# One-pass first gate/up products, and earlier or later lanes around them, in a hybrid decoder layer

## The chip, the cores and the metric

The kernel runs on one core of a Trainium2 chip. The metric is the time of one execution on the device in microseconds (us). The core has five engines that this text names as the profile does: PE (TensorE, matrix products), DVE (VectorE), ACT (ScalarE), POOL (GpSimd) and SP (SyncE, which here only issues DMAs). Each engine works through its own list of instructions in order, and waits on semaphores where an instruction needs another engine's result or a landed DMA. Results of PE arise in banks of PSUM, the accumulators' memory, which the kernel takes as tiles of 128x512 float32 (four for `mm`, three for `tr`, one for `ct`).

## The reference

The reference is one decoder layer on a sequence of 2048 tokens of 1024 numbers, in float32:

```python
hn = rms_norm(h, mix_pre_g)
proj = hn @ w_in                      # q, k, v and the convolution group's input u
attn_out = sliding_window_attention(q, k, v, attn_sinks, rel_bias)   # window 128, 8 query heads, 2 kv heads
conv_out = conformer_conv(u, ...)     # GLU, causal depthwise conv of width 31, layer norm, silu, @ w_conv_pw
mixed = concatenate([attn_out, conv_out]) @ w_out
h = h + rms_norm(mixed, mix_post_g)
hn = rms_norm(h, ffn_pre_g)
ff = (silu(hn @ w_gate) * (hn @ w_up)) @ w_down        # 2816 hidden columns
h = h + rms_norm(ff, ffn_post_g)
```

## The kernel before

**Tiles and groups.** The sequence is cut into four tiles of 512 tokens, numbered 0 to 3. Letters mark the stages: A is the input projection of a tile, B its attention, C the convolution and its tail, J a product of weights (w_conv_pw with the lower half of w_out, so that the convolution's output meets one matrix `w_join` instead of two), W the output projection with the norms behind it, H the turned and scaled input of the feed-forward part, F the gate and up products, G the down products with the last norm. F and G work on two groups of two tiles each (group 0: tiles 0 and 1; group 2: tiles 2 and 3), and their products are done by a Strassen scheme with seven block products instead of eight: of a group's input, B11 and B21 are the two halves of its first tile's columns, and T1 to T4 and B22 are sums and differences with the second tile.

**float32 by three products.** Every float32 operand is split into a rounded part and a rest: ACT copies the rounded part (`act(..., AF.Copy)`), and DVE or POOL subtracts it for the rest (`lo`). One block product with 512 inner terms is four times three matmuls of 128x128 by 128x512, twelve in all, in one PSUM bank.

**The first gate/up pass.** `stage_pre` does the Strassen terms that need only a group's first tile, while the second tile is still on its way. For each of PRE = 20 (group 0) or 16 (group 2) weight matrices, alternately of w_gate and w_up, there is a first half, product with B11, and a second half, product with B21. Before the change all first halves run, then all second halves: the result of a first half is copied by ACT to SBUF (`u`, L965) and stored to HBM (`keep`, L966, on ACT's DMA queue). For its second half it is loaded back (`fetch`, L926, on SP's queue, into one of two `gb` tiles), and ACT copies it into a fresh PSUM bank (`seed`, L941), onto which PE adds the twelve matmuls of the second half. Of a gate matrix, ACT then takes silu (L970), and of an up matrix DVE multiplies. The stored first halves are also needed later, in the pass `stage_p1`, which loads all of them again.

**What sets the order.** The main line (A0 to A3, then F and G of group 0, F and G of group 2) is written as generators that yield a cost in us of PE, and lanes beside it (lists of other generators, with the condition under which each may start) are advanced at the yields: a lane for attention, one for the convolution tails and J, one for W0 to W3, one for H (`lh`). Each engine's list comes out of this and of a reordering by a cost model. `lh.until("B21.0")` drives the H lane until a named operand is written.

**The lanes in the places that the change touches.** `stage_join` loads six pairs of matrices in turn into the one tile `wx`, and splits them, for eight plus four products. `stage_w(0, ...)` starts when A3 has started and the convolution tail C0 is done. `stage_h_plain` turns tile 0's (or 2's) normed rows by PE transposes into bank `tr`, of which there are three, shared with attention; it reads the rows by DMA from `hn_scr`, where the norm at the end of W stores them. `stage_h_sums` does the same with the second tile and forms T1 to T4 and B22 (S0 and S2 below); it is started at product PRE_S0 = 22 or PRE_S2 = 16 of the pass. The tails of the convolution, C2 and C3, which run in the pass G of group 0, load four rows of `y_scr` one by one, each just ahead of its turning on PE.

Of the kernel before, what the change touches and what calls it, by code (L numbers as in the profile page):

```python
# [25 lines left out]
P = 128  # L26
# [11 lines left out]
def layer_kernel(ctx, tc, x, xT, cols, rows, sinks, relb, onehot, w_in, w_pw, w_out, w_gate, w_up, w_down, out):  # L38
# [539 lines left out]
    def stage_tail(t):  # L578
        L = f"C{t}"
        lab[0] = L  # L580
        yt = t_("yt", (P, 4, 4 * P))
        ycs = []
        turn = turner(yt, ycs)
        for c in range(4):
            lab[0] = L
            y = f2("fc")
            nc.sync.dma_start(y, y_scr[c, :, t * T : (t + 1) * T])
            ycs.append(y)
            turn(c)
            yield 0.5  # L590
        yield from conv_tail(t, yt)
# [28 lines left out]

    def stage_join():
        lab[0] = "J0"
        right = []
        for k in range(4):
            raw = f4("wx", (P, 2, T))
            nc.sync.dma_start(raw, w_out[4 + k].rearrange("p (a b) -> p a b", a=2))
            yield JL
            for n in range(2):
                lab[0] = "J0"
                right.append(split_w(raw[:, n], "mid" if k < 2 else "chl"))  # L630
            yield 1.5
            lab[0] = "J0"
        for mp in range(2):
            pair_ = t_("yt", (P, 2, 2, T), F32R)
            raw = f4("wx", (P, 2, T))
            nc.sync.dma_start(raw, w_pw[2 * mp : 2 * mp + 2].rearrange("m p t -> p m t"))
            yield JL
            lab[0] = "J0"
            left = [split_w(raw[:, m], pair_[:, m]).rearrange("p a (k c) -> p a k c", c=P) for m in range(2)]
# [74 lines left out]
    def stage_w(w, spill, G, atag, htag, mtag, bank_of, norm=None):  # L714
# [13 lines left out]
        stage = t_("mb", (P, 2, T)) if w == 1 else None  # L728
# [14 lines left out]
        for gi in range(KC // G):  # L743
            aa = nxt
            for n in range(2):
                lab[0] = L
                if n == 0 and gi + 1 < KC // G:
                    if w == 1 and G * gi + G == 4:
                        ld.until("C1")
                        lab[0] = L  # L750
                    rows_next = load(gi + 1)
# [94 lines left out]
    def stage_h_plain(ws, ops, n, off):  # L846
        L = f"H{ws[0]}"
        for k in range(4):
            lab[0] = L
            b = turned(ws[0], k + off, tr, COLTAG[ws[0]][k] if ws[0] else "fa")  # L850
# [53 lines left out]
    def stage_pre(ws, ops, mid, keep, q0=0, q1=None):  # L904
        PRE = PRES[ws[0]]
        q1 = q1 or 2 * PRE
        L = f"F{ws[0]}"
        raws = {}
        wops = {}
        kept = {}  # L910

        def load(q):
            if q < q1 and q % 2 == 0:
                lab[0] = L
                half, m = divmod(q, PRE)
# [5 lines left out]

        def fetch(q):
            if PRE <= q <= q1:
                lab[0] = L
                kept[q] = f2("gb")
                nc.sync.dma_start(kept[q], keep[q - PRE if q < q1 else 0])  # L926

        def split(q):
            if q < q1:
# [5 lines left out]
        seeded = {}  # L935

        def seed(q):
            if PRE <= q < q1:
                lab[0] = L
                seeded[q] = mm()  # L940
                act(seeded[q], kept.pop(q), AF.Copy)  # L941

        load(q0)
        load(q0 + 2)
        for q in range(q0, q0 + 3):
            split(q)
        for q in range(q0, q1):
            half, m = divmod(q, PRE)
# [6 lines left out]
            if q + 2 == PRE:  # L955
                fetch(q + 2)
            lab[0] = L
# [3 lines left out]
            o = seeded.pop(q) if half else mm()  # L961
            product(o, wops.pop(q), ops[bn], not half)
            if not half:
                u = f2("fa")
                act(u, o, AF.Copy)  # L965
                nc.scalar.dma_start(keep[m], u)  # L966
            else:
# [7 lines left out]
        early[ws[0]] = kept.pop(q1)  # L975
# [321 lines left out]
    class Lane:  # L1297
# [36 lines left out]
        def until(self, name):  # L1334
            while name not in self.done:
                assert self.items, name
                n, gen, needs = self.items[0]
                assert not needs or needs(), n
                inlane[0] = True
                for c in gen:  # L1340
                    assert c is not None
                inlane[0] = False
# [15 lines left out]
    PRES = {0: 20, 2: 16}  # L1358
    POOL_LO = (3, 6)
# [3 lines left out]
    JL = 10  # L1363
# [24 lines left out]
    lw.add("W0", stage_w(0, True, 2, "x", "hl", "fa", mm), lambda: "A3" in started and "C0" in ld.done)  # L1388
# [139 lines left out]
```

## Time and profile before

| | us |
|---|---|
| time, median of 3 runs (range) | 1991.51 (1990.13 to 1993.91) |
| profiled execution: its time | 1997.53 |
| profiled execution: its span | 1995.6 |
| PE busy | 1940.2 (97%) |
| DVE busy | 1488.0 (75%) |
| ACT busy | 970.8 (49%) |
| POOL busy | 331.1 (17%) |

The profiled execution is one run with the hardware's recorder on; its span runs from the first to the last instruction, and its time has 1.9 us more. It was 6.0 us longer than the median of the three runs without a recorder. Busy time is the time in which an engine has an instruction in work; "idle before, releaser" says how long an engine stood still ahead of a group of instructions, and which instruction of which other engine, or which DMA, ended that. PEld is the loading of the weights for a matmul, which runs beside the matmul before. PEclk is the clock that PE was granted, as a share of the full one. In the trace, the first gate/up pass of group 0 runs from about 568.8 to 702 us, that of group 2 from 1343.5 to about 1440 us; W1 ends at 569, J, W0 and the attention lie before, and the tails C2 and C3 between 1015 and 1343 us.

### The profile page before, as it was taken

To read this page: it belongs to the slowest core of one execution; us is meant where nothing else is said; L and a number is where in the kernel's file an instruction comes from. 1 tells how busy PE (TensorE), PEld (TensorE's weight loads), DVE (VectorE), ACT (ScalarE), POOL (GpSimd) and SP (SyncE) were. 2 spreads that over 40 slices of the span, in tenths; PEclk is the share of its full clock that TensorE was granted. 3 is DMA by queue.
4 is the path that set the end of the run, shared out by engine and by line. 5 is a ranking of instruction groups with operands and counts; after the bars stand their busy time and mean duration, and the time that the engine had idled before them with its cause. 6 is when DMAs were issued, how large, how long until landed. Compare 5 with 4: busy or idle time off the path is not lost.

```text
span 1995.6 us, 26899 instructions
## 1 busy us (share of the span) xinstructions
PE 1940.2 (97%) x8730; PEld 1546.2 (77%) x8730; DVE 1488.0 (75%) x2679; ACT 970.8 (49%) x1910; POOL 331.1 (17%) x395
## 2 busy tenths in 40 slices
PE   8999999899999999999999999999899999999998
PEld 6877677667777788878878878778688888888886
DVE  5998989955884899988759985675866665555557
ACT  5355334456566643333355446476544333345443
POOL 6001311231111300000000020003523332311000
PEclk9999999999999999999999999999999999999999
DMA  8786654567859876787477687689834442366654
GB/s 311 256 310 217 219 167 143 186 214 253 276 176 332 298 253 239 233 278 260 162 266 245 231 280 270 195 303 353 307 139 169 169 153 101 126 220 212 211 185 159
DMA packets 234364, 452.99 MB, mean 227 GB/s; under 512 B 23496, under 2 KB 49264, under 8 KB 234224
## 3 DMA queue, kind: packets, MB, share of 16 engines
q1 hardware_dynamic: 212592, 415.63, 61.8%
q10 hardware_dynamic: 19392, 28.32, 3.9%
q0 software_dynamic: 2240, 7.34, 1.0%
q8 instruction: 68, 1.11, 0.2%
q14 instruction: 72, 0.59, 0.1%
HBM read 330.08 MB, written 121.12 MB: 226 GB/s over the span
## 4 chain that ended last, share of the span: by engine, by line
PE 76%; DMA 9%; DVE 8%; issue 3%; ACT 3%; POOL 1%; SPq 0%; ACTq 0%; DVEq 0%; POOLq 0%
PE mm@F L108 30%; PE mm@G L108 18%; PE mm@A L108 14%; PE mm@W L108 4%; PE tr@W L108 4%; PE tr@B L108 3%; DMA gb@F<-keeps 2%; DVE fc@C L85 1%; PE ct@J L108 1%; DVE mid@W L85 1%; DMA mixT<-fc@C 1%; DVE w@F L85 1%; DMA chl@F<-w_up 1%; DVE fa@F L85 1%; DVE chl@F L85 1%
## 5 line engine op out<-in xcount | busy, mean ns | idle before, releaser
L85 DVE SCALAR_TENSOR_TENSOR fc@C<-glu@C,colt,fc@C 128x512 f32<-128x512 f32 x480 | 367.9, 782 | 2.4
L108 PE MATMUL mm@F<-hl@H,w@F 128*128 128x512 f32 x1056 | 254.2, 390 | 4.3 <-ACT mm@F L941 4.3
L108 PE MATMUL mm@G<-hl@G,hl@G 128*128 128x512 f32 x924 | 227.4, 397 | 7.4 <-ACT mm@G L1232 2.9
L108 PEld LDWEIGHTS mm@F<-hl@H,w@F 128*128 128x128 f32 x1056 | 197.5, 188 | 47.0 <-ACT mm@F L941 6.2
L108 PE MATMUL mm@A<-hl@A,w@A 128*128 128x512 f32 x840 | 209.4, 398 | 2.6 <-DVE hl@A L85 1.3
L108 PEld LDWEIGHTS mm@G<-hl@G,hl@G 128*128 128x128 f32 x924 | 173.5, 190 | 46.5 <-ACT mm@G L1232 3.4
L108 PE MATMUL mm@G<-w@G,hl@G 128*128 128x512 f32 x876 | 199.7, 389 | 0.0
L814 ACT ACTIVATE w@F<-chl@F 128x512 fp32r<-128x512 f32 x220 | 135.0, 624 | 118.6 <-PE mm@F L108 112.8
L108 PEld LDWEIGHTS mm@G<-w@G,hl@G 128*128 128x128 f32 x876 | 164.3, 188 | 34.4 <-issue 0.3
L108 PEld LDWEIGHTS mm@A<-hl@A,w@A 128*128 128x128 f32 x840 | 156.8, 190 | 40.6 <-DVE hl@A L85 3.0
L85 DVE TENSOR_TENSOR w@F<-chl@F,w@F 128x512 fp32r<-128x512 f32 x198 | 145.2, 735 | 39.0 <-ACT w@F L814 38.8
L108 PE MATMUL mm@F<-mid@H,w@F 128*128 128x512 f32 x528 | 132.3, 394 | 7.9 <-ACT mm@F L941 7.3
L108 PE MATMUL mm@F<-p@H,w@F 128*128 128x512 f32 x528 | 130.6, 393 | 0.0
L108 PE MATMUL mm@F<-ql@H,w@F 128*128 128x512 f32 x528 | 127.1, 390 | 2.0 <-ACT w@F L814 2.0
L108 PE MATMUL mm@F<-x@H,w@F 128*128 128x512 f32 x528 | 126.8, 391 | 1.0 <-DVE x@H L85 0.9
L108 PEld LDWEIGHTS mm@F<-mid@H,w@F 128*128 128x128 f32 x528 | 98.1, 188 | 31.4 <-ACT mm@F L941 9.6
L108 PEld LDWEIGHTS mm@F<-ql@H,w@F 128*128 128x128 f32 x528 | 98.9, 188 | 23.0 <-ACT w@F L814 2.6
L108 PEld LDWEIGHTS mm@F<-p@H,w@F 128*128 128x128 f32 x528 | 100.1, 190 | 21.3 <-ACT at@F L1068 0.4
L108 PEld LDWEIGHTS mm@F<-x@H,w@F 128*128 128x128 f32 x528 | 98.3, 188 | 23.4 <-DVE x@H L85 1.4
L108 PE MATMUL mm@W<-w@W,hl@W 128*128 128x512 f32 x384 | 106.0, 415 | 7.4 <-ACT hl@W L723 5.6
L133 ACT ACTIVATE w@A<-raw@A 128x512 fp32r<-128x512 f32 x110 | 67.4, 626 | 73.9 <-PE mm@A L108 46.1
L85 DVE TENSOR_TENSOR w@G<-raw@G,w@G 128x512 fp32r<-128x512 f32 x73 | 51.2, 701 | 67.6 <-ACT w@G L814 66.6
(301 smaller groups left out, 3307.6 us busy)
## 6 DMA issues: line engine op xcount, KB each, us to landing
mids<-fa@F SPq DMA_DIRECT2D x154, 256.0 KB, 2.7
raw@A<-w_in SPq DMA_DIRECT2D x55, 512.0 KB, 4.4
w@A<-lo_in SPq DMA_DIRECT2D x84, 256.0 KB, 3.4
fc@G<-mids SPq DMA_DIRECT2D x77, 256.0 KB, 3.3
fa@G<-mids SPq DMA_DIRECT2D x75, 256.0 KB, 4.8
gb@F<-keeps SPq DMA_DIRECT2D x74, 256.0 KB, 4.5
w@W<-lo_out SPq DMA_DIRECT2D x48, 256.0 KB, 4.2
chl@F<-w_gate SPq DMA_DIRECT2D x22, 512.0 KB, 3.9
```

The lines of the kernel that those rows point to most:

```text
L85: r = op(*args, **kw)
L108: r = nc.tensor.matmul(*args, **kw)
L133: act(w[:, 0], raw, AF.Copy)
L814: act(w[:, 0], x, AF.Copy)
```

## The change

**The pass.** `TWO` says how many matrices of a group still have their halves in two rounds; it is 0 for both groups, so all go through in pairs: first half of matrix m, first half of m+1, second half of m, second half of m+1. The seed of a second half is no longer loaded from HBM: ACT copies it from the bank of the first half into a fresh bank, right behind the copy `u`. `u` is stored to HBM as before. The last `fetch`, of the first stored half, which `stage_p1` begins with, stays.

**J** loads its matrices one ahead, by turns into `wx` and a spare `mb` tile that W1 later uses. **W0** starts when J is done; C0 is asked for inside W0, where its second half begins. **H of group 0** turns its rows in bank `ct` (one bank, the convolution tail's) instead of `tr`. **C2 and C3** load their first two rows ahead of turning, and each further row one step ahead.

```diff
@@ -581,14 +581,30 @@
+        if t > 1:
+            yield from ahead(L, t, ycs)
         for c in range(4):
             lab[0] = L
+            if c == len(ycs):
+                y = f2("fc")
+                nc.sync.dma_start(y, y_scr[c, :, t * T : (t + 1) * T])
+                ycs.append(y)
+            turn(c)
+            if t > 1 and c < 2:
+                y = f2("fc")
+                nc.sync.dma_start(y, y_scr[c + 2, :, t * T : (t + 1) * T])
+                ycs.append(y)
+                yield 3
+            else:
+                yield 0.5
+        yield from conv_tail(t, yt)
+
+    def ahead(L, t, ycs):
+        for c in range(2):
             y = f2("fc")
             nc.sync.dma_start(y, y_scr[c, :, t * T : (t + 1) * T])
             ycs.append(y)
-            turn(c)
-            yield 0.5
-        yield from conv_tail(t, yt)
+        yield 6
 
...
+    spare = []
+
+    def spare_tile():
+        if not spare:
+            spare.append(t_("mb", (P, 2, T)))
+        return spare[0]
+
     def stage_join():
         lab[0] = "J0"
+        srcs = [w_out[4 + k].rearrange("p (a b) -> p a b", a=2) for k in range(4)]
+        srcs += [w_pw[2 * m : 2 * m + 2].rearrange("m p t -> p m t") for m in range(2)]
+        raws = {}
+
+        def load(i):
+            if i < len(srcs):
+                lab[0] = "J0"
+                raws[i] = spare_tile() if i % 2 else f4("wx", (P, 2, T))
+                nc.sync.dma_start(raws[i], srcs[i])
+
+        load(0)
+        load(1)
+        yield JL
         right = []
         for k in range(4):
-            raw = f4("wx", (P, 2, T))
-            nc.sync.dma_start(raw, w_out[4 + k].rearrange("p (a b) -> p a b", a=2))
-            yield JL
             for n in range(2):
                 lab[0] = "J0"
-                right.append(split_w(raw[:, n], "mid" if k < 2 else "chl"))
-            yield 1.5
+                right.append(split_w(raws[k][:, n], "mid" if k < 2 else "chl"))
+            yield JS
+            load(k + 2)
+            yield JS
+        for mp in range(2):
             lab[0] = "J0"
-        for mp in range(2):
             pair_ = t_("yt", (P, 2, 2, T), F32R)
-            raw = f4("wx", (P, 2, T))
-            nc.sync.dma_start(raw, w_pw[2 * mp : 2 * mp + 2].rearrange("m p t -> p m t"))
-            yield JL
-            lab[0] = "J0"
-            left = [split_w(raw[:, m], pair_[:, m]).rearrange("p a (k c) -> p a k c", c=P) for m in range(2)]
+            left = [split_w(raws[4 + mp][:, m], pair_[:, m]).rearrange("p a (k c) -> p a k c", c=P) for m in range(2)]
             yield 2
             for m in range(2):
                 for n in range(2):
@@ -725,7 +756,7 @@
-        stage = t_("mb", (P, 2, T)) if w == 1 else None
+        stage = spare_tile() if w == 1 else None
 
...
                 if n == 0 and gi + 1 < KC // G:
-                    if w == 1 and G * gi + G == 4:
-                        ld.until("C1")
+                    if w < 2 and G * gi + G == 4:
+                        ld.until(f"C{w}")
...
-            b = turned(ws[0], k + off, tr, COLTAG[ws[0]][k] if ws[0] else "fa")
+            b = turned(ws[0], k + off, tr if ws[0] else ct, COLTAG[ws[0]][k] if ws[0] else "fa")
...
-    def stage_pre(ws, ops, mid, keep, q0=0, q1=None):
-        PRE = PRES[ws[0]]
-        q1 = q1 or 2 * PRE
+    def stage_pre(ws, ops, mid, keep):
+        PRE, two = PRES[ws[0]], TWO[ws[0]]
         L = f"F{ws[0]}"
-        raws = {}
-        wops = {}
-        kept = {}
+        seq = [(m, half) for half in range(2) for m in range(two)]
+        for m in range(two, PRE, 2):
+            seq += [(m + j, half) for half in range(2) for j in range(2)]
+        raws, wops, kept, seeded = {}, {}, {}, {}
 
         def load(q):
-            if q < q1 and q % 2 == 0:
-                lab[0] = L
-                half, m = divmod(q, PRE)
+            if q < len(seq) and q % 2 == 0:
+                lab[0] = L
+                m, half = seq[q]
                 raw = t_("raw", (P, 2, T))
                 for j in range(2):
                     src, pr = MATS[m + j]
                     nc.sync.dma_start(raw[:, j], src[2 * pr][:, half * T : (half + 1) * T])
                     raws[q + j] = raw[:, j]
 
+        def stored(q):
+            return q == len(seq) or q < len(seq) and seq[q][1] and seq[q][0] < two
+
         def fetch(q):
-            if PRE <= q <= q1:
+            if stored(q):
                 lab[0] = L
                 kept[q] = f2("gb")
-                nc.sync.dma_start(kept[q], keep[q - PRE if q < q1 else 0])
+                nc.sync.dma_start(kept[q], keep[seq[q][0] if q < len(seq) else 0])
 
         def split(q):
-            if q < q1:
+            if q < len(seq):
                 lab[0] = L
                 raw = raws.pop(q)
                 wops[q] = split_f(raw, hl("w"))
                 lo(raw, wops[q], ws[0] and q % 2 == 1)
 
-        seeded = {}
-
         def seed(q):
-            if PRE <= q < q1:
-                lab[0] = L
-                seeded[q] = mm()
-                act(seeded[q], kept.pop(q), AF.Copy)
-
-        load(q0)
-        load(q0 + 2)
-        for q in range(q0, q0 + 3):
+            if q < len(seq) and stored(q):
+                lab[0] = L
+                seeded[seq[q][0]] = mm()
+                act(seeded[seq[q][0]], kept.pop(q), AF.Copy)
+
+        load(0)
+        load(2)
+        for q in range(3):
             split(q)
-        for q in range(q0, q1):
-            half, m = divmod(q, PRE)
+        for q, (m, half) in enumerate(seq):
             started.add(f"P{ws[0]}.{q}")
             bn = "B21" if half else "B11"
             if len(ops.get(bn, ())) < 4:
                 lh.until(f"{bn}.{ws[0]}")
             split(q + 3)
             load(q + 4)
-            if q + 2 == PRE:
+            if stored(q + 2) and not stored(q + 1):
                 fetch(q + 2)
-            lab[0] = L
             seed(q + 1)
             fetch(q + 3)
             lab[0] = L
-            o = seeded.pop(q) if half else mm()
+            o = seeded.pop(m) if half else mm()
             product(o, wops.pop(q), ops[bn], not half)
             if not half:
                 u = f2("fa")
                 act(u, o, AF.Copy)
                 nc.scalar.dma_start(keep[m], u)
+                if m >= two:
+                    seeded[m] = mm()
+                    act(seeded[m], o, AF.Copy)
             else:
...
-        early[ws[0]] = kept.pop(q1)
+        early[ws[0]] = kept.pop(len(seq))
...
                 assert not needs or needs(), n
+                was = inlane[0]
                 inlane[0] = True
...
-                inlane[0] = False
+                inlane[0] = was
...
     PRES = {0: 20, 2: 16}
+    TWO = {0: 0, 2: 0}
...
-    JL = 10
+    JL, JS = 10, 2
...
-    lw.add("W0", stage_w(0, True, 2, "x", "hl", "fa", mm), lambda: "A3" in started and "C0" in ld.done)
+    lw.add("W0", stage_w(0, True, 2, "x", "hl", "fa", mm), lambda: "A3" in started and "J" in ld.done)
```

The first place is in the pass of group 2, on ACT. Before, its rows are (`raw` is a weight matrix as loaded, `w` its split, `gb` a half that was loaded back, `fa` the copy to be stored, `keeps` the store in HBM):

```order
L941 ACTIVATE mm@F_2232_12930<-gb@F_2227_12907 128x512
L965 ACTIVATE fa@F_2220_12877<-mm@F_2219_12864 128x512
L814 ACTIVATE w@F_2221_12880<-raw@F_2218_12861 128x512
L966 DMA keeps_4791<-fa@F_2220_12877 128x512
L814 ACTIVATE w@F_2225_12901<-raw@F_2218_12861 128x512
L965 ACTIVATE fa@F_2224_12898<-mm@F_2223_12885 128x512
L966 DMA keeps_4791<-fa@F_2224_12898 128x512
L814 ACTIVATE w@F_2231_12927<-raw@F_2226_12904 128x512
L941 ACTIVATE mm@F_2238_12956<-gb@F_2228_12909 128x512
```

Now they are, in the same pass:

```order
L1003 ACTIVATE fa@F_2163_12632<-mm@F_2134_12502 128x512
L995 ACTIVATE fa@F_2168_12670<-mm@F_2167_12657 128x512
L999 ACTIVATE mm@F_2169_12673<-mm@F_2167_12657 128x512
L845 ACTIVATE w@F_2174_12696<-raw@F_2166_12654 128x512
L996 DMA keeps_4789<-fa@F_2168_12670 128x512
L845 ACTIVATE w@F_2177_12716<-raw@F_2175_12699 128x512
L995 ACTIVATE fa@F_2172_12691<-mm@F_2171_12678 128x512
L999 ACTIVATE mm@F_2173_12694<-mm@F_2171_12678 128x512
```

The seed (L941, from a `gb` tile) has become a copy from bank to bank (L999) that stands directly behind the copy to be stored (L995) of the same product.

The second place is the start of W0, on ACT. L479 is the exponentials of one block of the attention, eight instructions; `hl@W` is the rounded half of a row of W0's input. Before:

```order
L133 ACTIVATE w@W_623_3790<-raw@W_622_3788 128x512
L355 ACTIVATE fa@A_581_3593<-mm@A_580_3568 128x512
L133 ACTIVATE w@W_624_3794<-raw@W_622_3788 128x512
L479 ACTIVATE p@B_523_3287,sm@B_530_3333<-p@B_523_3287,sm@B_528_3328 128x128 x8
L723 ACTIVATE hl@W_593_3626<-fa@W_591_3622 128x512
L476 ACTIVATE sm@B_529_3330<-sm@B_529_3330 128x8
L723 ACTIVATE hl@W_594_3629<-fa@W_592_3624 128x512
L723 ACTIVATE hl@W_620_3782<-fa@W_595_3632 128x512
```

Now (L754 is what L723 was):

```order
L133 ACTIVATE w@W_612_3714<-raw@W_610_3708 128x512
L754 ACTIVATE hl@W_581_3566<-fa@W_579_3562 128x512
L390 ACTIVATE kz<-kz 128x2x128
L754 ACTIVATE hl@W_582_3569<-fa@W_580_3564 128x512
L133 ACTIVATE w@A_622_3758<-raw@A_621_3756 128x512
L754 ACTIVATE hl@W_608_3702<-fa@W_583_3572 128x512
L479 ACTIVATE p@B_533_3333,sm@B_540_3379<-p@B_533_3333,sm@B_538_3374 128x128 x8
```

The first three rounded halves of W0 stand ahead of the eight exponentials; before, they stood behind them.

The third place is the start of the pass of group 2, on PE. `ql@H` is the operand B11, `mid@H` is B21. Before, sixteen first halves follow each other, of which these are the first rows:

```order
L832 MATMUL tr@H_2179_12642<-ident,at@H_2178_12640 128x128 x4
L108 MATMUL mm@F_2155_12529<-ql@H_2022_11755,w@F_2150_12514 128x512 x3
L108 MATMUL mm@F_2155_12529<-ql@H_2029_11782,w@F_2150_12514 128x512 x3
L108 MATMUL mm@F_2155_12529<-ql@H_2033_11801,w@F_2150_12514 128x512 x3
L108 MATMUL mm@F_2155_12529<-ql@H_2043_11842,w@F_2150_12514 128x512 x3
L108 MATMUL mm@F_2171_12596<-ql@H_2022_11755,w@F_2151_12517 128x512 x3
```

Now the rows from the end of the second first half on are:

```order
L108 MATMUL mm@F_2149_12555<-ql@H_2041_11933,w@F_2128_12474 128x512 x3
L108 MATMUL mm@F_2167_12657<-ql@H_2025_11862,w@F_2148_12552 128x512 x3
L108 MATMUL mm@F_2167_12657<-ql@H_2029_11884,w@F_2148_12552 128x512 x3
L108 MATMUL mm@F_2167_12657<-ql@H_2037_11914,w@F_2148_12552 128x512 x3
L108 MATMUL mm@F_2167_12657<-ql@H_2041_11933,w@F_2148_12552 128x512 x3
L108 MATMUL mm@F_2134_12502<-mid@H_2139_12523,w@F_2129_12477 128x512 x3
L108 MATMUL mm@F_2134_12502<-mid@H_2143_12536,w@F_2129_12477 128x512
L108 MATMUL mm@F_2151_12571<-mid@H_2139_12523,w@F_2130_12480 128x512 x3
```

B21 is taken up after three first halves (36 matmuls) instead of after sixteen (192), and the first two second halves are interleaved by its four rows of operands.

## The prediction

> **What bounds the kernel now.** I read the page first: what share of the span PE works, and which lines make PE wait.
>
> ```profile
> span 1995.6 us, 26899 instructions
> PE 1940.2 (97%) x8730; PEld 1546.2 (77%) x8730; DVE 1488.0 (75%) x2679; ACT 970.8 (49%) x1910; POOL 331.1 (17%) x395
> ...
> L108 PE MATMUL mm@F<-hl@H,w@F 128*128 128x512 f32 x1056 | 254.2, 390 | 4.3 <-ACT mm@F L941 4.3
> L108 PE MATMUL mm@G<-hl@G,hl@G 128*128 128x512 f32 x924 | 227.4, 397 | 7.4 <-ACT mm@G L1232 2.9
> ...
> L108 PE MATMUL mm@F<-mid@H,w@F 128*128 128x512 f32 x528 | 132.3, 394 | 7.9 <-ACT mm@F L941 7.3
> ...
> L108 PE MATMUL mm@W<-w@W,hl@W 128*128 128x512 f32 x384 | 106.0, 415 | 7.4 <-ACT hl@W L723 5.6
> ```
>
> PE is busy for 97% of the span; 1995.6 - 1940.2 = 55.4 us are idle. The change leaves the number of matmuls as it is, so it can only win from these 55 us and from stretches in which PE is granted a lower clock. Two of the largest single releasers lie in lines that the change touches: the seeds (ACT L941), 4.3 us in group 0's pass and 7.3 in group 2's, and W0's operands (ACT L723), 5.6. Next the chain of waits of the whole span, for who stands behind the seeds:
>
> ```profile
> ACT mm@F L941 <- DMA gb@F<-keeps: 21.4, 15, 4.0
> ...
> PEld mm@F L108 <- ACT mm@F L941: 15.8, 11, 3.3
> ...
> ACT junk L792 <- DVE mid@W L85: 13.9, 6, 3.5
> ...
> PE mm@F L108 <- ACT mm@F L941: 11.5, 11, 2.8
> ...
> ACT fa@F L965 <- DVE mid@W L85: 5.0, 2, 3.4
> ...
> ACT hl@H L887 <- DVE chl@H L85: 3.8, 1, 3.8
> ...
> ACT mid@H L887 <- DVE chl@H L85: 2.1, 1, 2.1
> ```
>
> The columns are total us, count and the longest. ACT waits 21.4 us for the reloaded halves, and PE 11.5 us, in 11 waits, for ACT's seeds.
>
> **Part 1, the pass.** Removed are 36 loads of 256 KB (the page: 74 in all, 4.5 us each to land) from SP's queue, 9.4 MB. PE does not wait for DMA bandwidth as such, so I book them at nothing beyond the waits above. Products, splits and copies stay as many; the stores of `u` stay too.
>
> ```profile
> gb@F<-keeps SPq DMA_DIRECT2D x74, 256.0 KB, 4.5
> ```
> ```profile
> L941 ACT ACTIVATE mm@F<-gb@F 128x512 f32<-128x512 f32 x36 | 21.4, 597 | 23.3 <-DMA gb@F<-keeps 21.4 <-DMA out<-x@G 1.0 <-DMA wx@G<-h_scr 0.9
> L965 ACT ACTIVATE fa@F<-mm@F 128x512 f32<-128x512 f32 x36 | 21.0, 590 | 12.7 <-DVE mid@W L85 5.0 <-DMA h_scr<-mid@W 3.0 <-PE mm@F L108 2.3
> ```
> ```profile
> 1343.49 43.82 PE L108 MATMUL mm@F<-ql@H,w@F 128*128 128x512 f32 x192
> ```
>
> 192 matmuls in 43.82 us are 0.228 us each, so a product of twelve takes 2.74 us. The seed of product m now needs the end of m, and is used when product m+1 has run: ACT must do the copy `u` (0.59) and the seed within 2.74 us. A copy from bank to bank is in no row; the nearest is the seed from SBUF, 0.60, which I take (bounds 0.3 to 0.9: half as much either way changes nothing). Slack: 2.74 - 0.59 - 0.60 = 1.55 us. So the waits for DMA go, but not those in which ACT itself was late. How many are those? Of the timeline of ACT:
>
> ```profile
> 1414.60 0.63 ACT L887 ACTIVATE hl@H<-chl@H 128x512 fp32r<-128x512 f32 x1 [3.77 <-DVE chl@H L85]
> ...
> 1424.84 0.60 ACT L941 ACTIVATE mm@F<-gb@F 128x512 f32<-128x512 f32 x1 [2.67 <-DMA gb@F<-keeps]
> ```
> ```profile
> 655.00:670.00 15.00, 13.72 (x74) 11.15 (x73) 13.14 (x19) 13.24 (x25) 5.67 (x4) 1.00 1.05 357
> ...
> 1402.00:1420.00 18.00, 14.36 (x68) 10.87 (x66) 17.79 (x21) 12.48 (x24) 11.42 (x8) 1.00 0.98 330
> ```
>
> The windows give the stretch, and busy time of PE, PEld, DVE, ACT and POOL. Some seeds wait for their load (1424.84), others stand behind ACT instructions of H that wait for DVE (1414.60). Where H runs beside the pass, ACT is busy for 13.24 of 15 us and DVE for 17.79 of 18; that load stays. Between a gain of 11.5 (all waits go) and none (each comes back on ACT), I take two thirds, **-8.0**, since 21.4 us of ACT's waits ahead of its seeds name the load, and of the two waits for `chl`, 3.8 and 2.1, only what is over the slack can reach PE.
>
> **Part 2, W0.** PE's first matmul of W0 waited here:
>
> ```profile
> 353.41 0.39 ACT L479 ACTIVATE p@B<-p@B,sm@B 128x128 f32<-128x128 f32 x1
> ...
> 356.49 0.62 ACT L723 ACTIVATE hl@W<-fa@W 128x512 fp32r<-128x512 f32 x1
> ```
> ```profile
> 357.16 0.80 PE L108 MATMUL mm@W<-w@W,hl@W 128*128 128x512 f32 x1 [3.89 <-ACT hl@W L723]
> ```
> ```profile
> 353.00:357.20 4.20, 0.31 (x7) 0.10 (x3) 4.17 (x9) 4.20 (x21) 1.85 (x2) 0.87 0.84 260
> 357.20:363.00 5.80, 5.80 (x14) 4.54 (x15) 5.76 (x19) 1.28 (x4) 0.00 (x0) 0.51 0.67 246
> ...
> 1419.40:1422.20 2.80, 0.00 (x0) 0.00 (x0) 1.60 (x2) 2.30 (x4) 2.80 (x3) 1.00 0.93 312
> 1422.20:1427.00 4.80, 4.55 (x19) 3.43 (x20) 2.80 (x5) 2.17 (x5) 1.79 (x2) 1.00 1.01 362
> ```
>
> The rounded row `hl@W` stood behind eight exponentials; PE stood for 3.89 us and then ran 14 matmuls in 5.8 us at a clock of 0.51, where 14 x 0.228 = 3.2 would do: 2.6 us more. In the new order the rounded rows stand ahead of the exponentials. Who is late next? The exponentials, by the three copies of 0.62 ahead of them; attention has its own slack of many products. Bounds -6.5 (all) and 0 (the wait moves to another place of W0's start, whose loads of `mixT` also come earlier); nearest is the row itself, of which I take three quarters: **-5.0**. The trace also tells when the clock falls: after 3.89 us without a matmul it was 0.51, after the 2.8 us at 1419.40 it stayed at 1.00. The Trainium skill, "TensorE: Matmul & The Clock Gate", section on the HAM clock gate, says that an idle window of about 3.4 us halves the clock, which a similar time of work restores; the rows agree on both sides, and by that rule a wait of under some 3 us costs itself alone.
>
> **Part 3, B21 of group 2.** PE takes B21 after 36 matmuls, 36 x 0.228 = 8.2 us behind the pass's start at 1343.49, at 1351.7. When was its last operand there?
>
> ```profile
> 1343.82 0.62 ACT L855 ACTIVATE mid@H<-gb@H 128x512 fp32r<-128x512 f32 x1
> ...
> 1348.97 0.63 ACT L855 ACTIVATE mid@H<-gb@H 128x512 fp32r<-128x512 f32 x1 [0.75 <-DMA hn_scr<-mid@W]
> ```
> ```profile
> 1349.89 0.69 DVE L85 TENSOR_TENSOR mid@H<-gb@H,mid@H 128x512 fp32r<-128x512 f32 x1
> ...
> 1351.17 0.69 DVE L85 TENSOR_TENSOR mid@H<-gb@H,mid@H 128x512 fp32r<-128x512 f32 x1
> ```
>
> At 1351.9, so just too late even before; now two seeds of 0.6 us stand on ACT's list ahead of its last two rows, 1.2 us, and behind each of them DVE subtracts. The operand comes in four rows, used in turn, which helps. Bounds 0 and 6.5 (the wait at 353 with its slow clock); I take **+2.5**, a wait like the 2.8 us at 1419.
>
> **Part 4, the norm of W1 and S0.** H of the second tile begins at product 22 in both kernels. Before, the end of attention and H's transposes lay among the first products; now most of these lie ahead of W1's end, so product 22 comes some 22 x 2.74 = 60 us after it. The chain of the norm between the two took:
>
> ```profile
> 569.25 0.68 DVE L85 TENSOR_TENSOR mid@W<-mid@W,mm@W 128x512 f32<-128x512 f32 x1
> ```
> ```profile
> 585.52 0.53 POOL L162 TENSOR_TENSOR sm@W<-sm@W,sm@W 128x4 f32<-128x4 f32 x1
> ```
> ```profile
> 595.28 0.42 SPq L705 DMA_DIRECT2D gb@W<-rows  x1
> ```
> ```profile
> 610.35 1.28 DVE L85 TENSOR_TENSOR mid@W<-fa@W,mid@W 128x512 f32<-128x512 f32 x2
> 621.04 0.69 DVE L85 TENSOR_TENSOR mid@W<-at@W,mid@W 128x512 f32<-128x512 f32 x1 [1.44 <-DMA at@W<-x]
> ```
> ```profile
> 655.74 0.60 PE L832 MATMUL tr@H<-ident,fc@H 128*128 128x128 f32 x4
> ```
>
> From 569.9 to 655.7 are 85.8 us. Two pieces of it are waits for buffers: from 586.0 (the factor is there) to 595.28 the gain's load waits for a `gb` tile that H holds, 9.2; from 611.6 to 621.0 the next rows of x come through `at` tiles that attention also uses, 9.4. Without both the chain has 67 us, 7 over the room. The rest of it is paced by the lane's own yields, which denser products pass sooner. Between 0 and 85.8 - 60 = 26 I take **+2**, near the chain without its buffer waits.
>
> **The rest, at nothing.** H of group 0 in one bank: its transposes lie in W1, where PE has other matmuls; -1 to +4. J earlier: its splits stand on POOL ahead of two selections of attention, for which PE waited 4.40 us; that wait can go or grow by one split of 6.76 / 2 = 3.4 us.
>
> ```profile
> 217.18 1.97 PE L108 MATMUL tr@B<-p@B,vd@B 128*64 128x512 f32 x4 [4.40 <-POOL p@B L504]
> ```
> ```profile
> 208.29 6.76 POOL L135 TENSOR_TENSOR chl@J<-wx@J,chl@J 128x512 fp32r<-128x512 f32 x2 [5.09 <-ACT chl@J L133]
> ```
>
> C2 and C3: their rows come earlier and their turning later, in a stretch in which PE waits 7.4 us for other lanes; -3 to +3. Covered by the matmuls of G.
>
> **Sum.** -8.0 - 5.0 + 2.5 + 2.0 = -8.5 us. Against the profiled execution, 1997.5 (span and 1.9 us around it), that is 1989.0; it lies 6.0 over the median of the runs, 1991.5, and the same difference gives **1983.0**.
>
> **Rivals.**
> *Given back on ACT.* The seed now needs ACT within 1.55 us of its product's end, and ACT works in order. Each wait of ACT for H or the norm that is longer comes through: 3.4 - 1.55 and 3.8 - 1.55 and 2.1 - 1.55 are 4.7 us. For it speaks that `fa@F L965` waited for `mid@W`; against it that H's stretch loses half of its seeds, which now lie over the whole pass. Sum -3.8, 1987.7, within 0.2% of before (4.0 us, about what a measurement of this kernel can tell).
> *The norm late (slower).* If only the wait for `gb` goes, the chain has 85.8 - 9.2 = 76.6 us against 60: PE stands 16 us ahead of S0's transposes. Sum -8.5 - 2 + 16 = +5.5, 1997.0. From a chain of 60 + 10.5 = 70.5 us on, nothing is won. For it: 67 us is what rows leave; against: the lane's yields shrink with the room.
> *The slow clock at B21.* If part 3's wait reaches 3.9 us, the clock goes with it: 6.5 in place of 2.5, sum -4.5, 1987.0. This is the skill's clock-gate rule in this place; the row of 357.20 shows it.
> *Loads hidden anyway.* That the halves' loads cost nothing is excluded by 11.5 us of PE.
>
> **Chances.** The forecast 0.5; given back 0.13; norm late 0.27; slow clock 0.1. Faster is the forecast and the slow clock, 0.6; same 0.13; slower 0.27. The range: below, the full -11.5 and -6.5, 1973; above, the norm's case and 2 more, 1999. For the forecast alone it is 1974 to 1988.
>
> **What would show it.** No row of ACT with `gb@F<-keeps` in the passes, but PE's waits for the new seed line, in sum about 3.5 us; no wait of PE at the first `mm@W` and a clock of 1.00 behind it; a wait of 2 to 3 us at the first `mid@H` matmul of group 2; at most 2 at S0's first transpose. The prediction is wrong if ACT's waits for DVE reach PE in every pair, or if a wait of over 3.5 us stands at S0.

## The result and the profile after

The changed kernel is a little faster: a median of 1985.72 us (1978.12 to 1992.44, 22 runs) against 1989.80 us (1982.56 to 1995.78, 22 runs) of the kernel before. The ratio is 0.9982, with a 95% interval of 0.9972 to 0.9992; of 1990 us that is 3.6 us less (1.6 to 5.6). The forecast was 8.5 us less, and 1983.0 us.

The profiled execution after took 1989.5 us with a span of 1987.5, 8.1 us under the span before. That difference must be read with care, as the second trace of the unchanged kernel shows below. The page of the changed kernel, with the groups that answer to those of before:

```profile
span 1987.5 us, 26862 instructions
...
PE 1939.4 (98%) x8730; PEld 1546.7 (78%) x8730; DVE 1483.3 (75%) x2679; ACT 969.1 (49%) x1910; POOL 334.5 (17%) x395
...
L108 PE MATMUL mm@F<-hl@H,w@F 128*128 128x512 f32 x1056 | 257.4, 392 | 3.9 <-ACT mm@F L999 3.9
...
L108 PE MATMUL mm@F<-mid@H,w@F 128*128 128x512 f32 x528 | 133.3, 395 | 6.0 <-ACT fa@F L1108 3.5
...
L108 PE MATMUL mm@W<-w@W,hl@W 128*128 128x512 f32 x384 | 104.6, 412 | 0.8 <-ACT fa@A L355 0.8
```

PE now stands before `mm@W` for 0.8 us in place of 7.4, and no longer for ACT's `hl@W`. The first matmul of W0 follows the work before it with no wait behind ACT:

```profile
350.76 0.97 PE L108 MATMUL tr@B<-kz,ql@A 64*128 64x256 f32 x12 [0.64 <-DVE sm@B L460]
351.66 0.50 PE L108 MATMUL mm@W<-w@W,hl@W 128*128 128x512 f32 x1
```

Of the waits (total us, count, longest), those around the seeds:

```profile
ACT fa@F L995 <- PE mm@F L108: 24.7, 18, 3.8
...
PE mm@F L108 <- ACT mm@F L999: 5.1, 4, 1.9
...
PE ct@C L559 <- DMA fc@C<-y_scr: 2.6, 1, 2.6
...
PE mm@F L108 <- DVE mid@H L85: 1.5, 1, 1.5
```

No wait for reloaded halves is left in the pass. PE still waits 5.1 us in four waits for ACT's seeds, now copied from bank to bank (the copy took 0.591 us on average; 0.60 was assumed). Three of the four stand ahead of a second half, which needs its seed. The fourth, 1.24 us, stands ahead of the third first half of group 2, which takes no seed:

```profile
1345.78 3.06 PE L108 MATMUL mm@F<-ql@H,w@F 128*128 128x512 f32 x12 [1.24 <-ACT mm@F L999]
```

As the kernel is written, what it needs is a bank: there are four for `mm`, the first two matrices hold two each, and one comes free when a seed has been copied out of it. New beside these are the waits for a row of `y_scr` in a convolution tail, 2.6 us, and for B21 (`mid@H`). Waits also grew away from the lines that were changed: in the later pass `stage_p1` PE waits 3.5 us for ACT's L1108 and 2.7 us for its L1087, where the first trace of before lists 0.6 us and none, and the transposes `tr@W` wait 5.0 us in place of 2.7. What lies behind these was not followed up.

Why is ACT late? Its timeline and PE's at two of the four places:

```profile
574.52 0.39 ACT L479 ACTIVATE p@B<-p@B,sm@B 128x128 f32<-128x128 f32 x1
...
577.70 0.57 ACT L995 ACTIVATE fa@F<-mm@F 128x512 f32<-128x512 f32 x1
578.17 0.58 ACT L999 ACTIVATE mm@F<-mm@F 128x512 f32<-128x512 f32 x1
```
```profile
578.81 1.55 PE L108 MATMUL mm@F<-hl@H,w@F 128*128 128x512 f32 x5 [1.92 <-ACT mm@F L999]
```
```profile
618.04 2.19 ACT L830 ACTIVATE mid@W<-mid@W,sm@W 128x1024 f32<-128x1024 f32 x2 [2.89 <-POOL sm@W L162]
...
622.70 0.58 ACT L999 ACTIVATE mm@F<-mm@F 128x512 f32<-128x512 f32 x1
```
```profile
623.33 1.89 PE L108 MATMUL mm@F<-hl@H,w@F 128*128 128x512 f32 x7 [1.17 <-ACT mm@F L999]
```

At 574 eight exponentials of attention, and at 618 the four scalings of W1's norm, which themselves had waited 2.89 us for POOL, stand on ACT's list between a product and its seed. Both are longer than the 1.55 us that the seed has. The first of these waits cost more than its 1.92 us: the twelve matmuls behind it took 4.54 us, where 12 x 0.228 = 2.74 would do, and the granted clock from 578.81 to 583.30 was 0.63. The start of group 2's second halves:

```profile
1352.30 0.73 PE L108 MATMUL mm@F<-mid@H,w@F 128*128 128x512 f32 x2 [0.74 <-ACT mid@H L886]
1354.57 3.91 PE L108 MATMUL mm@F<-mid@H,w@F 128*128 128x512 f32 x9 [1.54 <-DVE mid@H L85]
```
```profile
1351.00:1354.60 3.60, 1.32 (x6) 0.47 (x4) 3.53 (x12) 3.54 (x10) 0.00 (x0) 1.00 1.03 367
1354.60:1358.60 4.00, 4.00 (x10) 2.93 (x10) 2.74 (x9) 0.67 (x3) 0.00 (x0) 0.57 0.97 310
```

B21's last rows are late, by 0.74 and 1.54 us, and behind them PE ran at a clock of 0.57: ten matmuls in 4.0 us, where 10 x 0.228 = 2.3 would do, 1.7 us more. The norm of W1, on the other hand, was in time for S0: its first transposes follow a product without a wait.

```profile
634.35 2.89 PE L108 MATMUL mm@F<-hl@H,w@F 128*128 128x512 f32 x12
637.07 0.60 PE L863 MATMUL tr@H<-ident,fc@H 128*128 128x128 f32 x4
```

### The profile page after: what moved, and what is told of

Same layout as the page of the kernel before. It is cut to its first block, busy times and chain, and to the rows that moved or that the text cites. A ratio compares the mean times of both kernels' runs of the same rounds, so it can differ in the third digit from the quotient of the medians.

```text
span 1987.5 us, 26862 instructions
## 1 busy us (share of the span) xinstructions
PE 1939.4 (98%) x8730; PEld 1546.7 (78%) x8730; DVE 1483.3 (75%) x2679; ACT 969.1 (49%) x1910; POOL 334.5 (17%) x395
## 4 chain that ended last, share of the span: by engine, by line
PE 76%; DMA 9%; DVE 9%; ACT 2%; issue 2%; SPq 1%; POOL 1%; DVEq 0%; ACTq 0%
PE mm@F L108 35%; PE mm@G L108 15%; PE mm@A L108 13%; PE mm@W L108 4%; PE tr@W L108 3%; PE tr@B L108 3%; DVE fc@C L85 3%; DMA mixT<-fc@C 1%; PE ct@J L108 1%; DMA wx@G<-h_scr 1%; DMA mids<-fa@F 1%; DMA at@W<-mixT 1%; DVE hl@G L85 1%; DMA td<-fc@G 1%; DVE mid@W L85 1%
## 5 line engine op out<-in xcount | busy, mean ns | idle before, releaser
L108 PE MATMUL tr@W<-w@W,ql@W 128*128 128x512 f32 x384 | 100.5, 402 | 5.6 <-ACT ql@W L754 5.0
```

The costliest lines, as they stand in the source:

```text
L108: r = nc.tensor.matmul(*args, **kw)
```

## The experiments

The theory at the outset was that two parts bring the time: the pass in pairs (seed waits gone, less what B21 costs) and the earlier start of W0. The rivals were that one of them alone does. Each kernel was measured beside the kernel before on the same chip. All results first, with 95% intervals (1 us is 0.0005; rows of different chips are compared through the kernel before); "lanes" are J, W0 and H of group 0 as changed, "tails" C2 and C3 as changed, "pairs" the pass as changed.

| kernel | lanes | tails | pass | ratio to before |
|---|---|---|---|---|
| e1 | no | no | pairs | 1.0004 (0.9989 to 1.0019) |
| e7 | no | yes | two rounds | 1.0008 (0.9995 to 1.0022) |
| e5 | yes | no | two rounds | 0.9972 (0.9958 to 0.9987) |
| e2 | yes | yes | two rounds | 0.9977 (0.9962 to 0.9993) |
| changed kernel | yes | yes | pairs | 0.9982 (0.9972 to 0.9992) |
| e8 | yes | no | pairs in group 0 alone | 0.9984 (0.9967 to 1.0000) |
| e3 | yes | no | pairs | 0.9940 (0.9924 to 0.9956) |
| e11, the same again | yes | no | pairs | 0.9956 (0.9941 to 0.9971) |
| e4 | yes | yes | pairs, first four of group 2 in two rounds | 1.0071 (1.0054 to 1.0089) |
| e12 | no | no | pairs in place | 0.9967 (0.9954 to 0.9980) |
| e9 | yes | no | pairs in place | 0.9911 (0.9891 to 0.9932) |
| e10 | yes | yes | pairs in place | 0.9903 (0.9884 to 0.9922) |

### The pass alone (e1)

`stage_pre` of the changed kernel in the kernel before, with this line added:

```diff
+    TWO = {0: 0, 2: 0}
```

> The kernel before with the new first gate/up pass alone (both groups in pairs, seeds copied from bank to bank); J, W0, H and the tails as before. Theory 'two parts': the waits of PE for seeds fall from 11.5 us to about 5, the wait for B21 in group 2 with its slow clock costs about 4 back, so this is 2 to 3 us faster than before, and the wait of 3.9 us with the slow clock at the first matmul of W0 stays. Theory 'pass alone': the whole difference of 4 us is here. Theory 'lanes alone': no difference, within 1 us of before.

It made no difference, 1.0004. The seeds' waits did fall, but others came:

```profile
PE mm@W L108 <- ACT hl@W L723: 5.8, 3, 3.9
PE mm@F L108 <- DVE x@H L85: 3.6, 1, 3.6
...
PE mm@F L108 <- ACT mm@F L968: 2.5, 3, 1.2
```

The waits of W0 stand as before (5.8 us). For seeds PE waits 2.5 us, and for B11 (`x@H`) 3.6 in place of 0.9, at the pass's start, where H still lies among the products with the old lanes; behind that wait the clock was 0.50 from 573 to 577 us. "Lanes alone" forecast this ratio; "two parts" forecast 2 to 3 us less, of which the interval (2.2 us less to 3.8 more) just leaves the lower end.

### The lanes with the pass in two rounds (e2)

```diff
-    TWO = {0: 0, 2: 0}
+    TWO = {0: 20, 2: 16}
```

> The changed kernel with the pass in two rounds again (all first halves, then all second halves with reloaded seeds); J, W0, H and the tails as changed. Theory 'two parts': the wait at W0's first matmul (3.9 us and 2.6 us of slow clock) is gone, PE's waits for reloaded seeds are there again, 10 us or more, and about 2.7 us of new waits in the tails: 2 to 4 us faster than before. Theory 'pass alone': no difference. Theory 'lanes alone': 4 us faster.

4.6 us faster than before: within its interval all that the whole change brings. With e1 this says that in the changed kernel the lanes carry the gain and the pairs add nothing that can be measured.

### The tails (e3, e5, e7, e8)

e3 is the changed kernel with

```diff
-        if t > 1:
-            yield from ahead(L, t, ycs)
         for c in range(4):
             lab[0] = L
-            if c == len(ycs):
...
-    def ahead(L, t, ycs):
-        for c in range(2):
             y = f2("fc")
             nc.sync.dma_start(y, y_scr[c, :, t * T : (t + 1) * T])
             ycs.append(y)
-        yield 6
+            turn(c)
+            yield 0.5
+        yield from conv_tail(t, yt)
```

> The changed kernel with the tails C2 and C3 as before (each row loaded just ahead of its turning). If the wait of 2.6 us for a row of y_scr at C2's turning belongs to the new order of loads, this is some 2.5 us faster than the changed kernel, 6 to 7 us faster than before. Rival: the waits in the down products are set by how all lanes fall together, and come elsewhere in G: as fast as the changed kernel within 1 us.

0.9940, and 0.9956 when measured again (e11): 5 to 8 us faster than the changed kernel. More than the wait of 2.6 us for `fc@C` went, so the first theory is right in sign and short in size. Is that the tails' own cost, and what is the pass worth without them? e7 is the kernel before with the new tails alone, e5 is e3 with the pass in two rounds, e8 is e3 with `TWO = {0: 0, 2: 16}`.

> The kernel before with the new tails C2 and C3 alone. Theory 'the tails cost by themselves' (a wait for a row at C2's turning, W2 and W3 later): 1.003 to 1.004 of before, 6 to 8 us slower. Rival 'they cost only with the pass in pairs', which asks for B21 eight products earlier than the pass in two rounds: within 2 us of before.

> The kernel with the tails C2 and C3 and the pass in two rounds as before, and J, W0 and H of group 0 as changed. Theory 'the pass is worth nothing': the pass alone measured 1.0004, so what remains without the tails' change comes from J, W0 and H: 0.994 of before, 11 us, as with the pass. Rival 'the pass pays once the tails are out of its way': about 0.998, and the pass brings 7 us on top.

> The kernel with the tails as before, J, W0 and H as changed, the pass in pairs for group 0 and in two rounds for group 2. If pairs help in group 2 (seed waits of 7 us in the trace of before), this is 3 to 6 us slower than the kernel with pairs in both groups (0.994 of before); if the pass is worth nothing, as fast as that, within 1.5 us.

Alone the tails cost 0.0008 (-0.0005 to +0.0022), under their forecast, and with the lanes and two rounds as little (e2 against e5): they cost much only with the pass in pairs. Without the tails the pairs bring 0.9972 - 0.9940 or - 0.9956 = 0.16 to 0.32%, 3 to 6 us, on top of the lanes. e11 alone would not show that; the mean of the two does, 4.8 us give or take some 3.6 (an estimate from the three intervals). Pairs in group 0 alone (0.9984) are no better than two rounds (0.9972), which points to group 2 for that gain; no run has pairs in group 2 alone. The rival "the pass pays once the tails are out of its way" forecast this, with 7 us.

Where the tails cost is seen at the start of group 2's pass. In e3 and e11 PE does not wait there, and in the changed kernel it waits 1.24, 0.74 and 1.54 us, with the slow clock behind. In the tail itself the changed kernel's 2.6 us for `fc@C` are followed by a clock of 0.65 over 4.9 us. Of the 7.0 us that the changed kernel needs more than e11 from G of group 0 to the end of group 2's pass (420.6 against 413.6), 3.0 are idle time of PE and 4.0 are busy time at a lower clock.

### B21 later (e4)

```diff
-    TWO = {0: 0, 2: 0}
+    TWO = {0: 0, 2: 4}
```

> The changed kernel with the first four matrices of group 2 in two rounds (four first halves, then their four second halves from HBM), the others in pairs: B21 of group 2 is taken up after four first halves and not after three. Theory 'B21 is late': the waits of 0.7 and 1.5 us and the slow clock behind them (1.8 us) go, some 4 us faster than the changed kernel. Rival: the four reloaded seeds wait for their loads as in the kernel before, and nothing is gained (within 1 us).

14 us slower than before, and not for a reason that either theory gave. PE, ACT's DMA queue and SP's:

```profile
1336.69 8.47 PE L108 MATMUL mm@F<-ql@H,w@F 128*128 128x512 f32 x36
1359.33 1.08 PE L863 MATMUL tr@H<-ident,fc@H 128*128 128x128 f32 x4 [14.17 <-DMA fc@H<-hn_scr]
```
```profile
1341.58 0.35 ACTq L833 DMA_DIRECT2D hn_scr<-mid@W  x1
```
```profile
1352.62 0.38 SPq L841 DMA_DIRECT2D fc@H<-hn_scr  x1
```

The reordering had put S2's transposes behind the third product, where PE arrives at 1345.2. The rows they turn were all stored by the norm of W3 at 1341.6, before that; but their load stands on SP's list behind others until 1352.6, and PE waits 14.17 us. So at this place it is the order of SP's list, not the norm, that made the rows late, and the changed kernel's order avoids it. The question of e4, what B21's lateness is worth, it does not answer.

### Before, once more (e6)

> The kernel before, unchanged, once more for a second trace. The first trace was of an execution of 1997.5 us, over every time measured of this kernel. Theory 'the seeds' waits are chance': PE's waits for reloaded seeds (11.5 us in the first trace) are below 8 us here, and the span shorter by as much. Rival: they are 10 to 12 us again, and the pass removes what is always there.

One execution of 1985.23 us, and in its trace:

```profile
span 1983.5 us, 26899 instructions
```
```profile
ACT mm@F L941 <- DMA gb@F<-keeps: 15.6, 14, 2.2
...
PE mm@F L108 <- ACT mm@F L941: 6.5, 6, 2.3
...
PE mm@W L108 <- ACT hl@W L723: 5.6, 3, 3.9
```

The same kernel has a span 12.1 us shorter, and PE waits 6.5 us in place of 11.5 for the seeds. The wait at W0 is the same 3.9 us in both. So the seeds' wait, behind which a load stands, changes from one execution to the next: the three other kernels with the pass in two rounds in both groups have 9.4 (e2), 10.9 (e7) and 6.7 us (e5) in their traces. The prediction took the highest of the five, from an execution of 1997.53 us, longer than all 22 above. The 3.9 us at W0, which ACT's order sets, stand in all five traces with the old lanes (both of before, e1, e7, e12). Not every wait that an engine ends is so steady: PE's wait for POOL's `p@B`, from which the prediction reads 4.40 us, is 1.1 us here.

### No seed copy (e9, e10, e12)

The second half can add to the bank of its own first half, once ACT has read that for the store. Three kernels do this, on e3, on the changed kernel, and on e1:

```diff
                 if m >= two:
-                    seeded[m] = mm()
-                    act(seeded[m], o, AF.Copy)
+                    seeded[m] = o
```

> The changed kernel with the tails as before and without the seed copies: the second half of a product adds to the bank of its first half as soon as ACT has copied that to SBUF. ACT loses 36 copies of 0.6 us, and PE needs ACT 0.6 us earlier in each pair less. Theory 'ACT's lateness is the price of the pairs' (three waits of 2.8, 1.9 and 1.0 us in the trace with copies): those waits shrink by 0.6 us or more each, 2 to 4 us faster than with copies. Rival 'the waits stand where ACT holds eight exponentials or four scalings of the norm ahead': about 2 us, and the order decides more than the copies: within 2 us of the same kernel with copies.

> The changed kernel, tails included, without the seed copies. If the tails cost in group 2 because ACT is late there (u, seed and H's copies in one row), the in-place form wins back 3 us or more of the changed kernel; if what they cost is that the norm of tile 3 ends later, B21's wait of 0.7 and 1.5 us with its slow clock stays, and this is within 2 us of the changed kernel (0.998 of before).

> The changed kernel with the tails as before, a second time, beside the two in-place kernels on one chip. The first measurement gave 0.994, 8 us under the changed kernel. Theory 'the tails cost 6 to 8 us where the pass is in pairs': 0.993 to 0.996 again. Rival: part of it was chance, and it comes out at 0.997, as the lanes without the pass.

> The kernel before with the pass in pairs in place (second half added to the bank of the first, no seed copies), and nothing else changed: J, W0, H and the tails as before. The pass in pairs with copies measured 1.0004 alone. Theory 'the copies took what the pairs brought': 0.992 to 0.995, the in-place form's gain with the other lanes (0.991 and 0.990) less the 4 to 6 us of W0 and J. Rival 'pairs need the changed lanes, H in its own bank above all': 0.998 or more, with a wait of PE for B11 of over 3 us at the start of the pass.

All three are faster than with copies: e12 at 0.9967 against 1.0004 (7 us), e9 at 0.9911 against 0.9940 and 0.9956 (6 to 9 us), e10 at 0.9903 against 0.9982 (16 us). e9 gained more than the 2 to 4 us that were expected of it, and e10 far more than the 3 at which its first alternative begins. e12 fell between its two theories (0.992 to 0.995, and 0.998 or more); PE's wait for B11 at the pass's start is 0.86 us there, not over 3. e9's and e10's medians are 1974.09 and 1973.26 us; they beat both kernels, and do not differ from each other. The first pass and the stretch from G of group 0 to the end of group 2's pass, in the windows of e11 (with copies) and e9 (length, then busy PE, PEld, DVE, ACT and POOL):

```profile
570.00:692.60 122.60, 118.53 (x530) 95.42 (x529) 79.86 (x123) 80.83 (x154) 27.80 (x38) 0.99 0.70 240
1011.40:1425.00 413.60, 402.35 (x1812) 328.87 (x1811) 332.14 (x557) 245.37 (x445) 70.39 (x100) 1.00 0.81 272
```
```profile
569.40:686.30 116.90, 116.40 (x531) 94.05 (x530) 84.57 (x124) 69.31 (x133) 30.07 (x38) 1.00 0.75 251
1002.80:1415.40 412.60, 400.78 (x1811) 327.22 (x1810) 319.58 (x553) 236.57 (x429) 66.37 (x100) 1.00 0.80 272
```

Group 0's pass loses 5.7 us: PE is idle for 0.5 in place of 4.1, and busy for 2.1 less, since the slow clock is gone with the wait (0.57 from 578 to 582 in e11, no such stretch in e9's pass); ACT is busy 11.5 us less (20 copies). The second stretch differs by 1.0 us only. Among e9's waits none of PE names a seed of the pass or the copy `u`. In e10, with the tails, PE takes up B21 of group 2 after four first halves, and the wait for it is 1.69 us, with the wait for `fc@C` about as in the changed kernel:

```profile
1329.09 11.22 PE L108 MATMUL mm@F<-ql@H,w@F 128*128 128x512 f32 x48 [0.90 <-DVE p@G L1224]
1340.14 3.33 PE L108 MATMUL mm@F<-mid@H,w@F 128*128 128x512 f32 x14
1345.17 1.20 PE L108 MATMUL mm@F<-mid@H,w@F 128*128 128x512 f32 x4 [1.69 <-DVE mid@H L85]
```
```profile
PE ct@C L559 <- DMA fc@C<-y_scr: 2.3, 1, 2.3
```

So most of the tails' own waits stay in e10, and yet it is as fast as e9. What is gone is for the larger part the slow clock: the clock is 1.00 behind the wait of 1.69 us. The same stretch in the changed kernel and in e10:

```profile
1012.80:1433.40 420.60, 406.30 (x1811) 330.78 (x1810) 321.66 (x557) 245.45 (x445) 66.26 (x100) 0.99 0.80 268
```
```profile
1009.60:1420.60 411.00, 399.77 (x1812) 327.48 (x1811) 320.55 (x554) 238.66 (x429) 68.36 (x100) 1.00 0.81 273
```

Of the 9.6 us, 3.1 are idle time of PE and 6.5 busy time, for the same matmuls. That the tails' cost goes with the copies is shown, and in size this is the first alternative of e10's expectation. How it goes is not: the in-place form takes away ACT's 36 copies and the second bank of each matrix at once, and the reordering moved B21 behind a fourth first half; no run parts these. e12 keeps the old lanes and gains 6.6 us, against 18 of e9; with 5.6 for the lanes (e5) the sum is 12, and whether pairs and lanes help each other beyond their sum is at the edge of what these intervals can tell.

## Why the prediction was right and where it was not

**Bound and direction.** PE bounds both kernels. Its idle time was 1995.6 - 1940.2 = 55.4 us before and 1987.5 - 1939.4 = 48.1 after, but in the second trace of before it was 1983.5 - 1934.7 = 48.8, so these traces do not show where the 3.6 us were won. The same 8730 matmuls kept PE busy for 1929.6 us (e9) to 1941.4 us (e4): the clock moves as much as the change was to bring. The kernel is faster, by 3.6 us where 8.5 were forecast. The time lies in the range, but so does the time before, and that the total came out near rests in part on luck: the largest term brought nothing, and the forecast stood on part 2.

**Part 1, the pass, -8.0: the step that failed.** The mechanism was seen (the load's waits go, ACT's stay), the size not. The 11.5 us came from one execution; the second trace shows 6.5. (Two thirds of 11.5 are 7.7, not 8.0.) And the slack of 1.55 us was weighed against waits of ACT for DVE alone, while eight exponentials and the norm's four scalings, which wait for nobody or for POOL, stood on ACT's list behind a product as well: 5.1 us of waits remained where 3.5 were forecast, and the slow clock behind the longest of them, 1.8 us, was in no term. Measured by substitution, the pairs with copies are worth nothing with the tails (0.9977 without, 0.9982 with), nothing alone (1.0004), and 3 to 6 us with the lanes and without the tails. The rival "given back on ACT" came nearest, with 3.8 us less: without the copies the changed kernel is 16 us faster. But of the waits that it named, those for DVE's `chl`, at most 0.79 us reached PE (at 677); the waits above came from the exponentials and the norm. The copies are as many as before, as was said; what changed is that before, a seed came from a half stored long ago, and now its copy can begin only when a product has ended, with the time of one other product to go.

**Part 2, W0, -5.0: right as far as shown.** The wait of 3.89 us is in all five traces with the old lanes, with a clock of 0.50 to 0.60 over the slowest 4 us behind it; with the new lanes the first `mm@W` waits 0.39 us at most. The lanes without the tails and with two rounds (e5) measured 0.9972, 5.6 us (2.6 to 8.4). J and H are in that figure; no run took W0 apart from them.

**Part 3, B21, +2.5: right in place, short in size.** 0.74 + 1.54 = 2.3 us of waits, and 1.7 us of slow clock that the forecast had given to a rival with a longer wait. The wait here was not one of 3.9 us but two short ones with two matmuls between them, in a stretch of 3.6 us in which PE was busy for 1.32. The Trainium skill, "TensorE: Matmul & The Clock Gate", section on the HAM clock gate, speaks of an idle window of about 3.4 us; these rows show the slow clock after a window that was only mostly idle. So the prediction's sentence that a wait of under some 3 us costs itself alone did not hold. The trace of before spoke against it already: behind waits of 2.66 us (at 1027.2), 1.75 (at 1168.1) and 1.44 (at 1310.1) the clock fell to 0.50, and behind the 2.8 us at 1419 it stayed at 1.00. The length of a wait does not tell by itself in these traces.

With the tails as before (e3, e11) PE does not wait for B21 at all, so this term comes with the tails and not with the pairs alone.

**Part 4, the norm of W1 and S0, +2: no wait at S0.** The transposes began some 68 us behind the last matmul of W1 (567.79 + 1.52), about the 67 that the forecast gave the chain; PE had products enough until then. The first load of its rows, at 647.25 before, was issued here:

```profile
625.86 0.38 SPq L841 DMA_DIRECT2D fc@H<-hn_scr  x1
```

A price showed elsewhere, the 1.17 us that PE waited at 623 for the seed behind the norm's scalings. The rival "norm late" did not happen here. e4 shows what late rows cost at the other group, 14.17 us, and there SP's list made them late.

**The rest, at nothing: wrong for the tails.** C2 and C3 cost 5 to 8 us beside the pairs (e3 and e11 against the changed kernel). The wait for `fc@C`, 2.6 us, was within the -3 to +3 that were given, but the step had not asked what a later W3 does to group 2's pass, where the same lane ends in the norm, whose scalings stand on ACT ahead of the first seed. There the changed kernel waits 3.5 us in three waits and pays 1.7 for the clock; that this cost goes with the seed copies is shown by e10. J and H of group 0 were not taken apart: the wait for POOL's `p@B` is gone, but it is down to 1.1 us in the second trace of before as well.

## What to carry to other kernels

When a copy that ran ahead of its use becomes one that must fit between two pieces of work of the bounding engine, count everything that the copying engine may have ahead of it in order, not only what it waits for; better still, see whether the copy is needed at all: letting PE add to the bank it had just filled was worth 16 us, where the whole change was worth 3.6. Before a wait of one trace is booked as a gain, take a second trace of the same kernel: here the wait that stood behind a load was 11.5 us in one and 6.5 in the other, the one set by ACT's order 3.9 in both. Compare the busy time of the bounding engine as well as its waits: for the same matmuls it differed here by up to 12 us. A change of several parts can be worth less or more than the sum of them, so take it apart and try the parts in pairs.

## What was not expected of the hardware

The slow clock after short waits: 0.57 over 4.0 us behind two waits of 0.74 and 1.54 us with two matmuls between them, and 0.63 over 4.5 us behind a single one of 1.92, while 1.69 us in e10 and 2.8 in the trace of before left it at 1.00. What decides is not shown. And the spread of one kernel from execution to execution: the kernel before took from 1982.56 to 1995.78 us in 22 runs (beside the experiments up to 2002.95), and two traces of it differ by 12.1 us in span, 5.0 of them in the seeds' waits alone.
